# Keys, values and query squares turned by VectorE blocks and a trip through memory instead of TensorE transposes

## The chip, the cores and the metric

The kernel runs on one core of a Trainium2 chip. The time is the device time in microseconds of one execution. Below, PE is TensorE's matmul stream and PEld its weight loads, DVE is VectorE, ACT is ScalarE, POOL is GpSimd and SP is SyncE, which issues most DMAs. Each engine works through its own list of instructions in order; an instruction that has to wait holds all that stand behind it on that engine.

## The reference: what is computed

One layer of a hybrid streaming encoder for 2048 prompt rows and 8 running streams of 16 rows, 1024 wide. After a norm and a product with `w_in`, one half of the mixer is a gated delta rule with 4 heads of 128, the other half a short gated convolution; then come the output product, a norm and a SwiGLU feed-forward part. The lines that matter here:

```
qkv, conv_new = causal_dwconv(qkv_in, conv_prev, conv_qkv_w)
qkv = jax.nn.silu(qkv.astype(jnp.float32))
q = l2norm(q by heads) * 128 ** -0.5 ;  k = l2norm(k by heads)
A = where(strict, (k * beta) @ k.T * decay, 0)           # per chunk and head
sol = triangular_solve(eye + A, [v * beta, k * beta * exp(g)])
S, o = scan over chunks: v_new = u - w @ S;  o = qg @ S + qk @ v_new
       S = S * exp(g_last) + k_tail.T @ v_new
```

The l2norm needs, for each row and head, the sum of squares of 128 numbers. The chunk steps need keys and values with rows on partitions, while the convolution produces them with channels on partitions, so a block of keys or values has to be turned.

## The kernel before

The work has a first phase (input product, convolutions, delta rule, gated convolution) and later ones (output product, feed-forward). The change touches the first phase alone.

The 17 row tiles of 128 rows form five groups of 4, 4, 3, 3 and 3 tiles (group 3 has the running streams' tile). For each group the main loop goes through 28 blocks of `w_in` columns in the order of `SEQS`: key, value, query and gate blocks of four heads each ("k", "v", "q", "z"), and the three kinds C, H and B of the gated convolution. A block is 24 matmuls into a PSUM bank (L326; the weights as high and low halves), issued in three thirds. After each third the loop runs the functions that are filed in the table `events` under that number, so a group has 84 places, 0 to 83. `PLAN` holds the numbers for the delta rule's steps: gate rates and sums, key norms, pair products, the solve's load and store, the levels a, b, c/d, and the chunk steps. `TURNS` holds, for kinds k, q and v and for each head, at which number the block is turned. The weights come as 1 MB loads (L296, from a split copy in memory) into three buffers: SP issues each when PE has released the buffer.

A finished block goes through `finish_block`: ACT copies the bank (R, L335) and makes the first convolution tap (acc, L367), DVE adds the other three (L330), ACT applies SiLU (L374: kT, qT or vraw). For k, q and v it returns one function `later`, filed under the number of `TURNS`. That function calls `turned` (L384): one TensorE transpose per tile into a PSUM bank (tbank). For k, `sumsq` squares the bank on ACT and sums on DVE (L390), and ACT copies the bank to `kt` (L409). For q only the squares' sums are taken. For v, ACT scales each tile by a row factor `rt` on its way to `vt` (L427).

The pair products (L597, L604) leave AU, from which DVE solves 32x32 triangular systems for all heads: it multiplies and subtracts small tiles (`pr`, L631, and `Ts`, L633) in 31 steps that shrink to 16 wide, and turns the result with two 32x32-block transposes (L638, L639: `utd`). Level a (L650) multiplies the turned blocks on TensorE, so it waits for L638 and L639. Levels b to d build the inverse further, and the chunk steps use it with `kt`, `vt` and the queries (from L768).

What stands between the steps of the solve on DVE (convolution taps, sums, copies for the next group's norm) is set by the order in which the program's scheduler places the instructions of all events on that engine.

## Time and profile before

| | us |
|---|---|
| median of 3 runs | 2420.13 (2420.04 to 2421.8) |
| profiled execution, its own time | 2421.49 |
| profiled execution, span of its instructions | 2419.5 |
| first phase, groups 0 to 4 start at about | 7, 189, 392, 546, 700 |
| PE busy in the span | 2402.4 |

The span is what the trace shows from the first to the last instruction; the execution's own time is 2 us longer. In rows of groups of instructions, the columns are line, engine, operation, names of output and input (buffer numbers left out), shape and count, then busy time, mean duration and idle time ahead of it. In timeline rows the first number is the start from the beginning of the span, the second the duration; "x8" is eight instructions in one row. PE's matmuls overlap in the pipeline: their own durations add up to more than the time they take.

### The profile page before, as it was taken

How to read it: one execution, taken by the hardware profiler on the slowest of the kernel's cores; microseconds unless marked ns; L12 is line 12 of the kernel's file. 1: busy time of each engine (PE TensorE's matmuls, PEld its weight loads, DVE VectorE, ACT ScalarE, POOL GpSimd, SP SyncE). 2: the span in 40 equal slices, each digit the busy share in tenths (PEclk: the TensorE clock that was granted, in tenths of full speed). 3: DMA queues.
4: the chain of work that ended last, by engine and by line, in shares of the span. 5: the costliest groups of instructions: out<-in, count | busy, mean ns of one | idle time of the engine just before them, and what ended most of it. 6: DMA issues, size and time to landing. Idle time of an engine off the chain costs nothing.

```text
span 2419.5 us, 39078 instructions
## 1 busy us (share of the span) xinstructions
PE 2402.4 (99%) x14222; PEld 2204.9 (91%) x14222; DVE 1603.4 (66%) x3042; ACT 1064.3 (44%) x2367; POOL 561.3 (23%) x667
## 2 busy tenths in 40 slices
PE   9999999999999999999999999999999999999998
PEld 7888889999989988899999999999999988888877
DVE  7875755746667466888788744546456555666787
ACT  6645545546445445543444423334333345333443
POOL 1211001001110000256555200000000035455663
PEclk9999999999999999999999999999999999999999
DMA  8774655766777668599888888888988844334376
GB/s 289 259 245 170 221 192 195 251 216 240 259 260 248 243 177 240 208 339 296 271 280 267 287 254 254 256 261 271 311 297 282 253 154 129 101 120 127 118 235 205
DMA packets 317063, 561.36 MB, mean 232 GB/s; under 512 B 95940, under 2 KB 198536, under 8 KB 299592
## 3 DMA queue, kind: packets, MB, share of 16 engines
q1 hardware_dynamic: 216864, 490.66, 61.1%
q10 hardware_dynamic: 99784, 67.17, 9.0%
q8 instruction: 112, 1.84, 0.3%
q0 software_dynamic: 224, 1.05, 0.1%
q14 instruction: 79, 0.65, 0.1%
HBM read 400.09 MB, written 158.70 MB: 231 GB/s over the span
## 4 chain that ended last, share of the span: by engine, by line
PE 93%; DVE 3%; ACT 1%; DMA 1%; POOL 1%; issue 1%; POOLq 0%; SPq 0%; DVEq 0%; ACTq 0%
PE fbank L1446 36%; PE dbank L326 25%; PE fbank L1637 17%; PE dbank L1200 4%; PE ftbank L1200 4%; PE tbank L384 1%; PE gbank L597 1%; PE gbank L604 1%; PE obank L776 1%; PE gbank L768 1%; PE gbank L790 1%; PE obank L798 1%; PE gbank L784 1%; DVE sA L1413 0%; PE gbank L701 0%
## 5 line engine op out<-in xcount | busy, mean ns | idle before, releaser
L1446 PE MATMUL fbank<-xh,fw 128*128 128x384 f32 (+1 forms) x3696 | 898.2, 326 | 2.7 <-ACT m L1479 1.7
L1446 PEld LDWEIGHTS fbank<-xh,fw 128*128 128x128 f32 x3696 | 651.2, 188 | 5.0 <-ACT m L1478 2.7
L326 PE MATMUL dbank<-hi,w 128*128 128x384 f32 (+1 forms) x2224 | 650.8, 363 | 0.2 <-ACT w L1008 0.2
L1446 PE MATMUL fbank<-xl,fw 128*128 128x384 f32 (+1 forms) x1848 | 602.1, 326 | 0.0
L326 PEld LDWEIGHTS dbank<-hi,w 128*128 128x128 f32 x2224 | 409.6, 188 | 40.4 <-issue 4.5
L1637 PE MATMUL fbank<-dw,as 128*128 128x512 f32 x1785 | 416.1, 391 | 2.5 <-ACT as L1617 1.1
L1637 PEld LDWEIGHTS fbank<-dw,as 128*128 128x128 f32 x1785 | 334.6, 188 | 76.9 <-ACT as L1617 1.5
L326 PE MATMUL dbank<-lo,w 128*128 128x384 f32 (+1 forms) x1112 | 396.7, 357 | 0.3 <-DVE lo L241 0.3
L1446 PEld LDWEIGHTS fbank<-xl,fw 128*128 128x128 f32 x1848 | 346.9, 188 | 0.0
L326 PEld LDWEIGHTS dbank<-lo,w 128*128 128x128 f32 x1112 | 209.3, 188 | 16.0 <-DVE lo L241 0.6
L1620 POOL TENSOR_TENSOR as<-ar,as 128x256 fp32r<-128x256 f32 (+1 forms) x202 | 173.8, 869 | 182.3 <-ACT as L1617 170.4
L1617 ACT CAST as<-ar 128x256 fp32r<-128x256 f32 (+1 forms) x287 | 119.0, 427 | 203.1 <-PE fbank L1637 154.9
L1590 DVE TENSOR_TENSOR acc<-acc,fbank 128x512 f32<-128x512 f32 x219 | 148.0, 683 | 86.7 <-PE fbank L1637 68.5
L1285 POOL TENSOR_TENSOR dw<-dr,dw 128x512 fp32r<-128x512 f32 x48 | 67.7, 1418 | 513.8 <-ACT dw L1283 513.4
L1421 ACT CAST fw<-rg 128x512 fp32r<-128x512 f32 x124 | 77.2, 622 | 223.3 <-PE fbank L1446 136.8
L330 DVE SCALAR_TENSOR_TENSOR acc<-R,vec,acc 128x512 f32<-128x512 f32 (+2 forms) x180 | 120.8, 673 | 26.8 <-ACT acc L367 20.9
L1494 DVE TENSOR_TENSOR c<-u,fbank 128x384 f32<-128x384 f32 (+1 forms) x66 | 34.9, 528 | 98.1 <-PE fbank L1446 98.1
L1490 DVE TENSOR_TENSOR m<-m,m 128x384 f32<-128x384 f32 (+1 forms) x44 | 23.1, 526 | 81.3 <-ACT m L1480 81.2
L1497 ACT ACTIVATE c<-c 128x384 f32<-128x384 f32 (+1 forms) x66 | 33.4, 506 | 95.3 <-DVE c L1496 95.3
L1422 POOL TENSOR_TENSOR fw<-rg,fw 128x512 fp32r<-128x512 f32 x44 | 65.9, 1499 | 34.1 <-ACT fw L1421 34.0
L1492 ACT ACTIVATE m<-fbank 128x384 f32<-128x384 f32 (+1 forms) x66 | 31.2, 473 | 94.0 <-PE fbank L1446 70.2
L359 POOL COPY hist<-R 128x3 f32<-128x3 f32 x60 | 18.4, 307 | 217.9 <-ACT R L335 172.3
(402 smaller groups left out, 3558.2 us busy)
## 6 DMA issues: line engine op xcount, KB each, us to landing
w<-wsplit SPq DMA_DIRECT2D x105, 1024.0 KB, 5.1
fw<-fsplit SPq DMA_DIRECT2D x188, 512.0 KB, 4.8
fsplit<-fw SPq DMA_DIRECT2D x94, 512.0 KB, 4.3
partd<-pt ACTq DMA_DIRECT2D x86, 384.0 KB, 6.3
rg<-in_w_gu SPq DMA_DIRECT2D x62, 512.0 KB, 4.3
wsplit<-w SPq DMA_DIRECT2D x28, 1024.0 KB, 4.9
ar<-partd SPq DMA_DIRECT2D x43, 384.0 KB, 3.2
wr<-in_w_in SPq DMA_DIRECT2D x32, 512.0 KB, 6.2
```

The source lines that it names most:

```text
L326: T.matmul(ps[:, :c], l[:, k, :], r[k][:, :c], start=(k == 0 and r is hi and l is wh), stop=(k == KD - 1 and l is wl))
L330: r = V.scalar_tensor_tensor(acc, raw(d), w[:, d:d + 1], acc, op0=ALU.mult, op1=ALU.add)
L1200: T.matmul(pss[n], m_[:, j, :], w_[k][:, n * 512:(n + 1) * 512], start=(k == 0 and ci == 0), stop=(k == KD - 1 and ci == 2))
L1285: e.tensor_tensor(out=w[1], in0=v, in1=w[0].bitcast(F32), op=ALU.subtract)
L1421: A.copy(w[:, 0], v)
L1422: e.tensor_tensor(out=w[:, 1], in0=v, in1=w[:, 0].bitcast(F32), op=ALU.subtract)
L1446: T.matmul(ps, w_[:, c], b_[k][:, :hw], start=(first and k == 0 and ci == 0), stop=(k == KH - 1 and ci == 2), skip_group_check=not first)
L1494: V.tensor_add(c21, u2, b3)
L1590: mark_d["V"] = V.tensor_tensor(out=dst if out is None else out, in0=dst, in1=ps, op=ALU.add)
L1617: ins = mark_d["A"] = A.copy(a[:, 0, :n], v)
L1620: mark_d["V" if e is V else "G"] = e.tensor_tensor(out=a[:, 1, :n], in0=v, in1=a[:, 0, :n].bitcast(F32), op=ALU.subtract)
L1637: ins = T.matmul(ps, a[:, x_, q * P:(q + 1) * P], w[y_], start=(start and q == 0 and ci == 0), stop=(q == c - 1 and ci == 2), skip_group_c ...
```

## The change

Three things are altered for each group.

*Keys and values.* `turn_out` lets DVE turn the block's 32x32 squares in place of a full transpose (STREAM_TRANSPOSE of the whole block, into `kt` or `vt`), and SP stores the result in four DMAs, one for each quarter of the partitions, to a scratch tensor `turnd` in memory, with runs of 32 floats (128 bytes) set so that the tensor holds rows by channels. `turn_in` loads it back with rows on partitions. Then `key_sums` squares on ACT and sums on DVE from `kt`, and `value_scale` scales `vt` in place on ACT. The three functions of a block have three numbers in `TURNS`, some 3 apart.

*Query squares.* `query_parts` turns the block's squares on DVE, squares it on ACT and sums runs of 32 on DVE into `pq`; `query_sums`, once per group, adds the four parts with four matmuls against small identities (`eyes`) into one bank, which DVE copies to `ssq`.

*Plan.* `turned`, `sumsq` and their TensorE transposes are gone. The numbers for the key norms move to 33, 31 and 24 (from 32, 26 and 17), group 1's chunk steps from 66 to 68.

```diff
@@ -40,14 +40,18 @@
         [16, 17, 18, *range(0, 4), *range(8, 12), *range(12, 16), *range(4, 8), *range(19, 28)],
         [*range(0, 4), *range(8, 12), *range(12, 16), *range(4, 8), *range(16, 28)])
 LATE = (*SEQS[0][:2], 7, 11, 19, 23, 27)
-PLAN = {0: (14, 20, 22, 26, 32, 36, 40, 50, (67, 69, 71), 75),
-        1: (16, 20, 23, 28, 26, 33, 38, 51, (56, 58, 60), 66),
-        2: (8, 14, 17, 22, 17, 28, 32, 47, (52, 55, 58), 63),
-        3: (8, 14, 17, 22, 17, 28, 32, 47, (53, 56, 59), 64),
-        4: (8, 14, 17, 22, 17, 28, 32, 47, (52, 55, 57), 62)}
-TURNS = ({"k": (19, 19, 31, 31), "q": (43, 43, 55, 55), "v": (52, 52, 64, 64)},
-         {"k": (17, 20, 23, 26), "q": (33, 33, 39, 39), "v": (55, 55, 61, 61)},
-         {"k": (14, 14, 17, 17), "q": (28, 28, 31, 31), "v": (46, 46, 52, 52)})
+PLAN = {0: (14, 20, 22, 26, 33, 36, 40, 50, (67, 69, 71), 75),
+        1: (16, 20, 23, 28, 31, 33, 38, 51, (56, 58, 60), 68),
+        2: (8, 14, 17, 22, 24, 28, 32, 47, (52, 55, 58), 63),
+        3: (8, 14, 17, 22, 24, 28, 32, 47, (53, 56, 59), 64),
+        4: (8, 14, 17, 22, 24, 28, 32, 47, (52, 55, 57), 62)}
+TURNS = ({"k": ((11, 14, 17), (14, 17, 20), (19, 22, 26), (25, 28, 31)), "q": ((33,), (38,), (55,), (61,)),
+          "v": ((46, 49, 52), (52, 55, 58), (58, 61, 64), (64, 67, 70))},
+         {"k": ((17, 19, 22), (20, 22, 25), (22, 25, 28), (25, 27, 30)), "q": ((29,), (32,), (35,), (38,)),
+          "v": ((52, 55, 58), (55, 58, 61), (58, 61, 64), (61, 63, 65))},
+         {"k": ((8, 11, 14), (11, 14, 17), (14, 17, 20), (17, 20, 23)), "q": ((21,), (24,), (27,), (30,)),
+          "v": ((43, 46, 49), (46, 49, 52), (49, 52, 55), (52, 55, 58))})
+QSUM = (66, 42, 34)
 TLS = True
 O_SPLIT = 7
 NPD, NPT, NPG = 3, 2, 2
@@ -129,6 +133,7 @@
     mixo = [dram.tile([P, H, P], F32, name=f"mixo{t}") for t in range(NT)]
     mixs = [dram.tile([P, 4, len(g) * P], F32, name=f"mixs{gi}") for gi, g in enumerate(GROUPS)]
     wsplit = [dram.tile([P, 2, KD, P], F32, name=f"wsplit{j}") for j in range(28)]
+    turnd = {(kind, gi): dram.tile([H, len(g) * P, P], F32, name=f"turn{kind}{gi}") for kind in "kv" for gi, g in enumerate(GROUPS)}
     hTd = [dram.tile([4 * len(g), 32, D] if gi else [D, len(g) * P], F32, name=f"hTd{gi}") for gi, g in enumerate(FGROUPS)]
     partd = [[dram.tile([len(g) // 2, P, 7, len(c) // 2, P], F32, name=f"partd{gi}_{ch}") for ch, c in enumerate(FCHUNKS)]
              for gi, g in enumerate(FGROUPS)]
@@ -378,17 +383,47 @@
             if rb is not None:
                 flush()
 
-        def turned(src, n):
-            ps = tbank()
-            for i in range(n):
-                T.transpose(ps[:, i * P:(i + 1) * P], src[:, i * P:(i + 1) * P], ident)
-            return ps, ps[:, :n * P].rearrange("p (t d) -> p t d", d=P)
-
-        def sumsq(ps, n, ss, h):
+        def turn_out(g, kind, h, src):
+            n, dst = g["n"], g[kind + "t"][:, h]
+            V.transpose(dst[:, :n].rearrange("p t d -> p (t d)"), src[:, :n * P])
+            for a in range(4):
+                r = slice(32 * a, 32 * a + 32)
+                with tc.issue_after(wloads[-1].ins):
+                    nc.sync.dma_start(out=turnd[kind, g["gi"]][h, :, r].rearrange("(j c) f -> c j f", c=32),
+                                      in_=dst[r, :n].rearrange("c t (j f) -> c (t j) f", f=32))
+
+        def turn_in(g, kind, h):
+            with tc.issue_after(wloads[-1].ins):
+                nc.sync.dma_start(out=g[kind + "t"][:, h, :g["n"]], in_=turnd[kind, g["gi"]][h].rearrange("(t p) d -> p t d", p=P))
+
+        def key_sums(g, h):
+            n = g["n"]
             sq = cp.tile([P, W1], F32, tag="cs", name="sq")
-            A.activation(sq[:, :n * P], ps[:, :n * P], AF.Square)
-            V.tensor_reduce(out=ss[:, :4 * n].rearrange("p (t h) -> p h t", h=H)[:, h], in_=sq[:, :n * P].rearrange("p (t d) -> p t d", d=P),
-                            axis=AX.X, op=ALU.add)
+            A.activation(sq[:, :n * P].rearrange("p (t d) -> p t d", d=P), g["kt"][:, h, :n], AF.Square)
+            V.tensor_reduce(out=g["ssk"][:, :4 * n].rearrange("p (t h) -> p h t", h=H)[:, h],
+                            in_=sq[:, :n * P].rearrange("p (t d) -> p t d", d=P), axis=AX.X, op=ALU.add)
+
+        def query_parts(g, h, src):
+            c = g["n"] * P
+            if not h:
+                g["pq"] = small.tile([P, 4, MAXT, H], F32, tag="pq", name="pq", bufs=1)
+            qb = cp.tile([P, W1], F32, tag="vraw", name="qb", bufs=NKV)
+            V.transpose(qb[:, :c], src[:, :c])
+            A.activation(qb[:, :c], qb[:, :c], AF.Square)
+            V.tensor_reduce(out=g["pq"][:, :, :g["n"], h].rearrange("p j t -> p t j"),
+                            in_=qb[:, :c].rearrange("p (t j f) -> p t j f", j=4, f=32), axis=AX.X, op=ALU.add)
+
+        def query_sums(g):
+            m = 4 * g["n"]
+            ps = bank()
+            for j in range(4):
+                T.matmul(ps[32 * j:32 * j + 32, :m], eyes, g["pq"][:, j, :g["n"]].rearrange("p t h -> p (t h)"), start=True, stop=True)
+            V.tensor_copy(g["ssq"][:, :m], ps[:, :m])
+
+        def value_scale(g, h):
+            for i in range(g["n"]):
+                v = g["vt"][:, h, i]
+                A.activation(v, v, AF.Copy, scale=g["rt"][:, 4 * i + h:4 * i + h + 1])
 
         def sm(nm, w=4 * MAXT):
             return small.tile([P, w], F32, tag=nm, name=nm)
@@ -403,29 +438,18 @@
                 conv_qkv(tiles, 4 + h, ps, o, rb)
                 g["kT"].append(o)
 
-                def later():
-                    tb, t3 = turned(o, n)
-                    sumsq(tb, n, g["ssk"], h)
-                    A.copy(g["kt"][:, h, :n], t3)
-                return later
+                return [lambda: turn_out(g, "k", h, o), lambda: turn_in(g, "k", h), lambda: key_sums(g, h)]
             if kind == "q":
                 o = gp.tile([P, W1], F32, tag="qT", name="qT", bufs=H)
                 conv_qkv(tiles, h, ps, o, rb)
                 g["qT"].append(o)
 
-                def later():
-                    tb, _ = turned(o, n)
-                    sumsq(tb, n, g["ssq"], h)
-                return later
+                return [lambda: query_parts(g, h, o)]
             if kind == "v":
                 raw = cp.tile([P, W1], F32, tag="vraw", name="vraw", bufs=NKV)
                 conv_qkv(tiles, 8 + h, ps, raw, rb)
 
-                def later():
-                    _, t3 = turned(raw, n)
-                    for i in range(n):
-                        A.activation(g["vt"][:, h, i], t3[:, i], AF.Copy, scale=g["rt"][:, 4 * i + h:4 * i + h + 1])
-                return later
+                return [lambda: turn_out(g, "v", h, raw), lambda: turn_in(g, "v", h), lambda: value_scale(g, h)]
             if kind == "z":
                 src = ps[:, :c]
                 if rb is not None:
@@ -885,6 +909,7 @@
                 at(pairs + 3 * (i // 2) + i % 2 - 1, decay_scale, g, i)
                 at(pairs + 3 * (i // 2), pair_keys, g, i)
                 at((52, 42, 33)[min(gi, 2)] + 3 * (i // 2), pair_queries, g, i)
+            at(QSUM[min(gi, 2)], query_sums, g)
             at(load, solve_load, g)
             for b in range(4):
                 at(load + 2 + 3 * b * (store - load - 2) // 13, solve, g, range(8 * b, min(31, 8 * b + 8)))
@@ -1038,6 +1063,10 @@
             if k == 2:
                 fetch()
                 held = [mark["cast"], mark["rest"]]
+        eyes = gp.tile([P, 32], F32, name="eyes")
+        for b in range(4):
+            r = slice(32 * b, 32 * b + 32)
+            G.tensor_copy(eyes[r], ident[r, r])
         gps = gate_matmuls(raws, c)
         matmuls(firsts[2], pending[2][1:], hi, lo, c, range(6))
         with tc.issue_after(ins.ins):
@@ -1104,10 +1133,9 @@
                     if not early:
                         matmuls(ps, w, hi, lo, c, ks)
                     if s == 2:
-                        later = finish_block(j, ps, g)
-                        if later:
-                            kind, h = BLOCKS[j]
-                            events.setdefault(TURNS[min(gi, 2)][kind][h], []).insert(0, later)
+                        kind, h = BLOCKS[j]
+                        for t, f in zip(TURNS[min(gi, 2)].get(kind, ((),) * 4)[h], finish_block(j, ps, g) or ()):
+                            events.setdefault(t, []).insert(0, f)
                         if gi or slot not in (2, 3):
                             with tc.issue_after(mark["rb"].ins), tc.issue_after(mark["E"].ins) if not gi and slot < 2 else ExitStack():
                                 fetch()
```

The order of instructions on the engines changes with it. Three places follow; in each the first list is from before, the second from the changed kernel.

ACT in group 2, where the value blocks are finished: `vraw` is the SiLU of a value block, `vt` the scaling of a turned one (three tiles per head), `cs` a copy for the gated convolution, `xt` squares for the next group's norm.

```order
L374 ACTIVATE vraw<-acc 128x384
L261 ACTIVATE xt,xss<-xt 128x512 x2
L427 ACTIVATE vt<-tbank,rt 128x128 x6
L335 COPY R<-dbank 128x384
L367 ACTIVATE acc<-dbank,vec 128x384
L374 ACTIVATE vraw<-acc 128x384
L441 COPY cs<-dbank 128x384
L374 ACTIVATE vraw<-acc 128x384
```

```order
L266 ACTIVATE xt,xss<-xt 128x512 x2
L340 COPY R<-dbank 128x384
L372 ACTIVATE acc<-dbank,vec 128x384
L379 ACTIVATE vraw<-acc 128x384
L426 ACTIVATE vt<-vt,rt 128x128 x3
L465 COPY cs<-dbank 128x384
L379 ACTIVATE vraw<-acc 128x384
```

The first scaling of a value block, which waited for PE's bank, now waits for the first `turn_in` load, and still stands ahead of the last value block's SiLU.

DVE in group 2, the end of the solve up to its two transposes:

```order
L631 TENSOR_TENSOR pr<-As,Ts 128x96
L330 SCALAR_TENSOR_TENSOR acc<-R,vec,acc 128x384
L633 TENSOR_TENSOR Ts<-Ts,pr 128x8x12
L330 SCALAR_TENSOR_TENSOR acc<-R,vec,acc 128x384
L631 TENSOR_TENSOR pr<-As,Ts 128x91
L633 TENSOR_TENSOR Ts<-Ts,pr 128x7x13
L631 TENSOR_TENSOR pr<-As,Ts 128x78
```

```order
L655 TENSOR_TENSOR pr<-As,Ts 128x108
L657 TENSOR_TENSOR Ts<-Ts,pr 128x9x12
L655 TENSOR_TENSOR pr<-As,Ts 128x96
L657 TENSOR_TENSOR Ts<-Ts,pr 128x8x12
L655 TENSOR_TENSOR pr<-As,Ts 128x91
L388 STREAM_TRANSPOSE vt<-vraw 128x384
L657 TENSOR_TENSOR Ts<-Ts,pr 128x7x13
L655 TENSOR_TENSOR pr<-As,Ts 128x78
```

The fourth value block's transpose, which needs the SiLU from the ACT list above, stands seven steps before the solve's end; the other three stand at earlier steps of the same solve.

DVE in group 3, the last rows of the solve (`u` is the product of the first C and H blocks):

```order
L631 TENSOR_TENSOR pr<-As,Ts 128x16
L633 TENSOR_TENSOR Ts<-Ts,pr 128x16
L638 STREAM_TRANSPOSE utd<-Ts 128x32x16
L639 STREAM_TRANSPOSE utd<-utd 128x512
L450 TENSOR_TENSOR u<-cs,dbank 128x256
L456 TENSOR_TENSOR u<-cs,dbank 128x8x16
```

```order
L474 TENSOR_TENSOR u<-cs,dbank 128x256
L480 TENSOR_TENSOR u<-cs,dbank 128x8x16
L657 TENSOR_TENSOR Ts<-Ts,pr 128x4x14
L481 COPY sch<-u 128x16
L655 TENSOR_TENSOR pr<-As,Ts 128x45
L657 TENSOR_TENSOR Ts<-Ts,pr 128x3x15
L655 TENSOR_TENSOR pr<-As,Ts 128x30
L335 SCALAR_TENSOR_TENSOR acc<-u,vec,acc 128x400
L657 TENSOR_TENSOR Ts<-Ts,pr 128x2x15
L335 SCALAR_TENSOR_TENSOR acc<-u,vec,acc 128x400
L655 TENSOR_TENSOR pr<-As,Ts 128x16
L657 TENSOR_TENSOR Ts<-Ts,pr 128x16
```

The product `u`, which reads the H block's bank, and two of its taps moved ahead of the solve's last steps and its transposes.

## The prediction

> **What bounds the kernel now.** I read the page first, then the waits of TensorE (PE) in the first phase, then the timelines round the places where the change takes work away.
>
> ```profile
> span 2419.5 us, 39078 instructions
> PE 2402.4 (99%) x14222; PEld 2204.9 (91%) x14222; DVE 1603.4 (66%) x3042; ACT 1064.3 (44%) x2367; POOL 561.3 (23%) x667
> PEclk9999999999999999999999999999999999999999
> PE 93%; DVE 3%; ACT 1%; DMA 1%; POOL 1%; issue 1%; POOLq 0%; SPq 0%; DVEq 0%; ACTq 0%
> ```
>
> PE is busy 99% of the span, at full clock in every slice, and holds 93% of the chain of waits. The change lies in the first phase, five groups. By group (core line left out; columns: PE, PEld, DVE, ACT, POOL busy, clock, DMA share, GB/s):
>
> ```profile
> 7.00:189.00 182.00, 180.94 (x1115) 149.60 (x1116) 143.53 (x284) 107.97 (x186) 27.98 (x41) 1.00 0.75 259
> 189.00:392.00 203.00, 203.00 (x1314) 171.62 (x1312) 122.48 (x284) 104.96 (x242) 16.23 (x40) 1.00 0.53 194
> 392.00:546.00 154.00, 153.91 (x1149) 150.86 (x1149) 92.72 (x246) 78.61 (x204) 15.43 (x42) 1.00 0.66 230
> 546.00:700.00 154.00, 152.85 (x1150) 145.75 (x1150) 98.86 (x291) 76.70 (x200) 20.47 (x58) 1.00 0.71 247
> 700.00:860.00 160.00, 159.66 (x1181) 154.04 (x1180) 98.80 (x259) 78.98 (x186) 11.99 (x35) 1.00 0.71 247
> ```
>
> The groups begin at about 7, 189, 392, 546 and 700 us. In each, PE is idle for at most 1.2 us, while VectorE (DVE) is busy 60 to 79% and the DMA engines 53 to 75%. So an instruction taken off PE shortens the phase, unless PE then waits for another engine. PE's waits from 8 to 865 us, the longest first:
>
> ```profile
> PE gbank L845 <- ACT qT L842: 0.8, 1, 0.8
> PE gbank L527 <- DVE gg L519: 0.4, 1, 0.4
> ```
>
> Little is waited for; the next question is how near the others are to being waited for.
>
> **The change part by part.** *Removed from PE: 204 transposes (L384).* One shows 0.27 us, but they overlap, so I take the distance from the first of a set to the next instruction's start:
>
> ```profile
> 746.89 0.82 PE L384 MATMUL tbank<-cst,qT 128*128 128x128 f32 x6
> 747.55 0.72 PE L597 MATMUL gbank<-kT 128*128 128x128 f32 x5
> ```
>
> Six take 0.66 us, 0.11 each: 204 x 0.11 = **-22.4 us**, 48 of them (5.3) in groups 0 and 1 each and 36 (4.0) in the others. (By the Trainium skill, "VectorE: DVE Perf Modes", The three transpose paths, a 128x128 transpose costs TensorE 390 ns and VectorE 311; the distance here is less than a third of the first, so the figure is not used.)
>
> *Added to PE: four small matmuls per group for the query sums.* Nearest rows:
>
> ```profile
> L527 PE MATMUL gbank<-gg,masks x10: 175/258/285, 49.8 to 725.5; 128*128 128x16 f32 x4, 128*128 128x12 f32 x4, 128*128 128x8 f32 x2
> 483.43 0.95 PE L650 MATMUL gbank<-utd,AU 32*32 32x32 f32 x48
> ```
>
> Between 0.02 us each (48 small ones in 0.95) and 0.26 (alone): 0.1 to 1.0 us per group. I take 0.5, so **+2.5 us** (0.5 to 5).
>
> *Where PE can be made to wait.* Level a (L650) reads what DVE's triangular solve leaves (transposes L638, L639). The end of L638 against PE's start of L650, groups 0 to 4 (DVE rows, then PE rows; group 2's PE row is above):
>
> ```profile
> 145.26 1.17 DVE L638 STREAM_TRANSPOSE utd<-Ts 128x512 f32<-128x512 f32 x1
> 318.42 1.13 DVE L638 STREAM_TRANSPOSE utd<-Ts 128x512 f32<-128x512 f32 x1
> 482.14 1.14 DVE L638 STREAM_TRANSPOSE utd<-Ts 128x512 f32<-128x512 f32 x1
> 632.54 1.16 DVE L638 STREAM_TRANSPOSE utd<-Ts 128x512 f32<-128x512 f32 x1
> 787.18 1.12 DVE L638 STREAM_TRANSPOSE utd<-Ts 128x512 f32<-128x512 f32 x1
> ...
> 148.50 1.20 PE L650 MATMUL gbank<-utd,AU 32*32 32x32 f32 x64
> 320.73 0.95 PE L650 MATMUL gbank<-utd,AU 32*32 32x32 f32 x48
> 634.48 0.69 PE L650 MATMUL gbank<-utd,AU 32*32 32x32 f32 x32
> 788.45 0.95 PE L650 MATMUL gbank<-utd,AU 32*32 32x32 f32 x48
> ```
>
> Slack: 2.07, 1.18, 0.15, 0.78, 0.15 us. In two groups there is none, and DVE is full just ahead of it. The change puts DVE work into this solve; the prices:
>
> ```profile
> 460.00:475.00 15.00, 15.00 (x91) 14.97 (x90) 14.16 (x45) 5.99 (x16) 1.11 (x6) 1.00 0.74 269
> L639 DVE STREAM_TRANSPOSE utd<-utd x5: 674/711/712, 146.9 to 788.3; 128x512 f32<-128x512 f32 x5
> L390 DVE TENSOR_REDUCE ssq<-sq x20: 544/554/689, 101.6 to 755.0; 128x3 f32<-128x384 f32 x12, 128x4 f32<-128x512 f32 x8
> ```
>
> A 128x512 transpose is 0.71, about 0.6 back to back; I scale a 128x384 one to 0.53. No idle time takes them in: DVE is busy 14.16 of the 15 us ahead of the join.
>
> Group 2 (and 4): four value transposes, 2.1 us, and a copy and two small operations, 0.3, enter; the solve starts 0.85 earlier, since the query reduces no longer stand ahead; PE arrives 0.9 earlier (12 transposes less, matmuls added). Late: 2.4 - 0.85 + 0.9 - 0.15 = 2.3 us, on DVE's work alone.
> Group 1: two transposes 1.2 and a copy against two reduces 1.4, PE 1.9 earlier, slack 1.2: 0.7 to 1.1.
> Group 0: six transposes 3.9, a weight remainder 1.2 and an output pair 1.3 enter, two reduces and a tap (2.1) leave, so +4.5 with the copy; PE comes 3.0 earlier (32 transposes less, 0.5 added), slack 2.07: 5.4. And three key transposes now stand ahead of gg, for which PE already waited 0.4: +2.0. Together 7.4.
> Group 3: the first H block's product u and its two taps now stand ahead of the solve's last transpose, and that block ends right before level a. Before, they came after:
>
> ```profile
> 634.66 0.42 DVE L450 TENSOR_TENSOR u<-cs,dbank 128x256 f32<-128x256 f32 x1 [0.22 <-PE dbank L326]
> 637.54 1.30 DVE L330 SCALAR_TENSOR_TENSOR acc<-u,vec,acc 128x400 f32<-128x400 f32 x2 [0.49 <-ACT acc L458]
> ```
>
> From the block's end at 634.4: u to 635.2, ScalarE's (ACT) product 0.7, the last tap to 637.3, the transpose 1.2: level a at 638.5, 4 us after 634.48. With the rest, 4.3 to 5.
>
> *The round trip through memory.* A turned value block is stored in four pieces of 128-byte runs, loaded back, and scaled by ACT (L426). In group 2 ACT's first scale stands ahead of the copy cs and of the last value block's SiLU; DVE's fourth value transpose waits for that SiLU, and the rest of the solve stands behind it. So a DMA landing enters the chain to PE. Before, at that place (ACT, then DVE):
>
> ```profile
> 474.07 1.66 ACT L427 ACTIVATE vt<-tbank,rt 128x128 f32<-128x128 f32 x6 [0.52 <-PE tbank L384]
> 479.60 0.48 ACT L441 COPY cs<-dbank 128x384 f32<-128x384 f32 x1 [2.60 <-PE dbank L326]
> 479.98 0.53 ACT L374 ACTIVATE vraw<-acc 128x384 f32<-128x384 f32 x1
> 479.20 0.24 DVE L631 TENSOR_TENSOR pr<-As,Ts 128x78 f32<-128x78 f32 x1
> ```
>
> The same kind of store stands later in this trace (128-byte runs), with four on SyncE (SP) in a row; then a load of the size wanted:
>
> ```profile
> L1231 SPq DMA_DIRECT2D hTd<-ht x24: 318/564/2863, 873.7 to 931.4; - x24
> DMA to landing us min/median/max: 3.1/4.3/5.5
> 873.71 4.02 SPq L1231 DMA_DIRECT2D hTd<-ht  x4
> xk<-in_xT SPq DMA_DIRECT2D x18, 192.0 KB, 5.0
> ```
>
> The first value transpose ends at about 469.6, three thirds of a block before the scale of 474.07. Lower bound: issues 4 x 0.32, landing 3.1, load issue 0.3 and 3.1: back at 477.4, before the scale's slot near 478 (three thirds of a block, 4.4 us, after the first scale of before), nothing lost. Upper bound: issues 4.0, landing 4.3, load 5.0 and 0.3: 483.2. Then three scales 0.83, cs 0.38, SiLU 0.53, transpose 0.53, and the 4.1 us of solve from 479.20 to 483.28: L638 would end at 489.6, and PE, there at 482.5, waits 7. I take the middle of 2.3 and 7, rather to the low side since the store here is 96 KB and not 128: **4** in groups 2 and 4, **5** in group 3, where the late H block covers part. The Trainium skill ("DMA: Bandwidth & Descriptors", Specifications) states that transfers under 512 bytes are read-modify-written and miss the line rate. The trace speaks against a large effect: the 128-byte stores land in 4.3 us where the 192 KB load takes 5.0. By the same page's fixed 2.0 us per DMA (Anatomy of one DMA) the trip would be about 6 us and hidden; this trace's own minimum is 3.1 for one of the two.
>
> *Other additions, at nothing:* the key path. Its stores and loads are further ahead of their users; if late, the key sums delay the norms by as much. The weight loads share SP:
>
> ```profile
> w<-wsplit SPq DMA_DIRECT2D x105, 1024.0 KB, 5.1
> SPq L296 <- PE dbank L326: 372.8, 78, 8.2
> ```
>
> SP waits 4.8 us on average for PE before it issues one, two blocks ahead of its use; four stores ahead of it cost up to 4.0. The waiting covers it; without that cover each late load costs PE the excess. ACT loses 20 copies and gains squares of the same size.
>
> **Sum.** 2421.5 (the profiled execution; its span is 2419.5) - 22.4 + 2.5 + stalls (7.4 + 1.0 + 4 + 5 + 4 = 21.4) = 2423.0. The runs' median, 2420.13, is 1.4 lower than the profiled execution: **2422 us**, no change that can be told. Within 0.2% is 2415.3 to 2425.0, about what a measurement of this kernel tells from no change.
>
> **Rivals.** *The cover holds (faster).* Loads come back at the minimum and DVE's added work falls into gaps; only group 3's wait, fixed by its order, stays: 2420.1 - 22.4 + 2.5 + 4.3 = 2405. For it: DVE idles 40% of groups 2 to 4 as a whole. Against it: slack 0.15 at the join, where DVE is full. With half of the stalls, 10.7, it is 2411.
> *The round trip decides (slower).* Upper bounds of it: 7 in groups 2, 3 and 4; in group 0, where the DMA share is highest, 12, since there too the scale of one value block stands ahead of another's SiLU; 3 in group 1: 36 us, 2420.1 - 22.4 + 2.5 + 36 = 2436. It decides from a landing of the first scale's load later than about 478 in group 2, each microsecond costing one in each of four groups. For it: landings of 4.3 and 5.0 as medians. Against: their minimum of 3.1.
> *The weights run late (slower).* Where the stores of two heads, 8.0 us of SP, stand ahead of one weight load, they exceed SP's mean wait of 4.8 by 3.2; at half of the ten such pairs of value heads that is 16 us on the forecast, 2438. SP's 372.8 us of waiting and the two blocks of lead speak against it. That the change does not do what it says I give no room: the transposes are gone from PE's list.
>
> **How the numbers follow.** Forecast 0.35 (2415 to 2428; 0.27 of it within 0.2%, 0.02 faster, 0.06 slower); cover holds 0.32; round trip decides 0.28; weights late 0.05. Faster 0.34, same 0.27, slower 0.39. Two in ten left out at the ends: 2403 to 2436; the forecast's own range is 2415 to 2428.
>
> **What would show it.** Right: no L384 for keys, values and queries on PE, five query-sum sets under 1 us; PE waits at level a on DVE's transposed block of 4 us or more in groups 0, 2, 3 and 4, and near 1 in group 1; ahead of it DVE idle at the fourth value transpose for ACT, and ACT idle before the value scale for the DMA. Wrong: level a without waits; a value load that lands before its slot; waits of the main matmuls for weights.

## The result, and the profile after

The changed kernel takes 2456.49 us in the median of 4 runs (2454.6 to 2462.89) against 2420.39 for the kernel before (2420.04 to 2421.8): a ratio of 1.0153, 95% interval 1.0133 to 1.0173. It is 36 us slower. The forecast was no change, 2422, with a range of its own of 2415 to 2428 and, with the rivals, of 2403 to 2436; the result lies above both.

The page of the changed kernel, the rows that answer to those of before (span, busy time, clock, the chain by engine):

```profile
span 2456.3 us, 39073 instructions
PE 2399.6 (98%) x14058; PEld 2196.7 (89%) x14058; DVE 1632.5 (66%) x3107; ACT 1062.7 (43%) x2347; POOL 562.2 (23%) x671
PEclk9999999999999999999999999999999999999999
PE 84%; DVE 6%; ACT 3%; DMA 3%; issue 2%; POOL 1%; SPq 0%; POOLq 0%; DVEq 0%; ACTq 0%
```

PE holds 84% of the chain where it held 93%. The clock row shows 9 in every slice, as before; a slice is 61 us long and 9 stands for anything from 90% up, so this row cannot show what follows. PE's waits from 8 to 900 us (total, times, longest):

```profile
PE gbank L674 <- DVE utd L662: 15.9, 4, 6.1
PE gbank L420 <- DVE pq L413: 5.3, 1, 5.3
PE gbank L621 <- DVE AU L622: 4.7, 3, 2.1
PE dbank L331 <- DMA w<-wsplit: 4.7, 6, 1.7
PE gbank L420 <- DVE dt L629: 2.8, 3, 1.0
PE gbank L551 <- issue: 2.3, 1, 2.3
PE tbank L749 <- ACT o L744: 2.0, 1, 2.0
```

L674 is level a, L420 the query sums' matmuls, L621 the pair products, L551 the gate sums, L331 the blocks. With four small ones the list comes to 40.1 us; before, it came to 2.5. The stretches of the five groups as they lay before, in the columns of before (the last three numbers are PE's clock, the DMA share and GB/s; the changed kernel's groups start up to 28 us later, so the stretches only add up to the phase):

```profile
7.00:189.00 182.00, 170.07 (x1003) 138.92 (x1002) 144.00 (x282) 97.74 (x155) 23.36 (x38) 0.95 0.82 273
189.00:392.00 203.00, 198.22 (x1267) 166.53 (x1266) 124.93 (x288) 103.52 (x234) 17.87 (x40) 1.00 0.65 216
392.00:546.00 154.00, 146.13 (x1050) 139.81 (x1049) 93.47 (x248) 79.01 (x195) 14.63 (x39) 0.97 0.68 226
546.00:700.00 154.00, 146.71 (x1040) 142.09 (x1039) 98.12 (x284) 75.84 (x199) 18.36 (x50) 0.98 0.77 257
700.00:900.00 200.00, 191.48 (x1410) 180.02 (x1410) 125.21 (x326) 90.65 (x217) 17.06 (x49) 0.99 0.76 250
```

There is a second loss beside the waits: **the granted clock**, 1.00 in all five stretches before, is now 0.95, 1.00, 0.97, 0.98 and 0.99. Length times what is missing gives 9.1 + 0 + 4.6 + 3.1 + 2 = 18.8 us. Part of these stretches lies over a wait and costs nothing there. A block's matmuls on both sides of the 5.3 us wait in group 0, from PE's timeline:

```profile
147.34 0.39 PE L331 MATMUL dbank<-lo,w 128*128 128x512 f32 x1
153.28 0.31 PE L420 MATMUL gbank<-pq,eyes 128*32 128x16 f32 x8 [5.33 <-DVE pq L413]
154.97 0.63 PE L331 MATMUL dbank<-lo,w 128*128 128x512 f32 x1
```

The same matmul shows 0.39 us ahead of the wait and 0.63 behind it. Level a in the five groups, whose starts before stand in the prediction:

```profile
159.95 1.54 PE L674 MATMUL gbank<-utd,AU 32*32 32x32 f32 x64 [1.97 <-DVE utd L662]
335.02 1.20 PE L674 MATMUL gbank<-utd,AU 32*32 32x32 f32 x64 [0.94 <-DVE rh L223]
504.03 1.49 PE L674 MATMUL gbank<-utd,AU 32*32 32x32 f32 x48 [4.85 <-DVE utd L662]
661.54 1.06 PE L674 MATMUL gbank<-utd,AU 32*32 32x32 f32 x32 [6.08 <-DVE utd L662]
821.95 0.99 PE L674 MATMUL gbank<-utd,AU 32*32 32x32 f32 x48 [3.05 <-DVE utd L662]
```

Against 148.50, 320.73, 483.43, 634.48 and 788.45 they come 11.4, 14.3, 20.6, 27.1 and 33.5 us later: the loss grows by 11.4, 2.8, 6.3, 6.5 and 6.4 from one to the next. Of the solve's two last transposes, level a waits for the first alone (L638 before, L662 here): in group 4 it starts at 821.95, 0.15 us after L662's end (820.72 and 1.08), while the second, which began at 821.83 and takes 0.71, still runs. The books: waits 40.1 - 2.5 = +37.6, transposes -22.4, sums' matmuls about +1.2 (five sets of 0.24), clock at most +18.8. That is +35 for the first phase; the first feed-forward matmul starts at 1074.0 us against 1038.9, 35.1 later, and the rest of the 36.8 us of span is behind it. Where half clock lies over a wait it is counted twice here, some 4 us, so about 4 of the 35 us are left without an account.

The chain through memory in group 2, drawn in the prediction, is there. SP, ACT, DVE, in order of time:

```profile
485.78 2.05 SPq L392 DMA_DIRECT2D turnv<-vt  x4
489.93 4.18 SPq L392 DMA_DIRECT2D turnv<-vt  x4
494.22 0.41 SPq L397 DMA_DIRECT2D vt<-turnv  x1
...
497.29 0.99 ACT L426 ACTIVATE vt<-vt,rt 128x128 f32<-128x128 f32 x3 [4.22 <-DMA turnv<-vt]
498.54 0.52 ACT L379 ACTIVATE vraw<-acc 128x384 f32<-128x384 f32 x1
...
499.10 0.58 DVE L388 STREAM_TRANSPOSE vt<-vraw 128x384 f32<-128x384 f32 x1 [2.16 <-ACT vraw L379]
```

The first block's load is issued 8.4 us after its first store, behind the second block's four stores. ACT waits 4.2 us, and its first scaling starts 11.5 us after the first store's issue; the profile names the landing of a store as what ended the wait, and the load, issued at 494.22, is the other candidate. DVE then waits 2.2 us for the last SiLU. Whether that is what the change costs is for the experiments.

### The profile page after: what moved, and what is told of

Read it like the earlier page. It is cut to its first block, busy times and chain, and to the rows that moved or that the text cites. A ratio compares the mean times of both kernels' runs of the same rounds, so it can differ in the third digit from the quotient of the medians.

```text
span 2456.3 us, 39073 instructions
## 1 busy us (share of the span) xinstructions
PE 2399.6 (98%) x14058; PEld 2196.7 (89%) x14058; DVE 1632.5 (66%) x3107; ACT 1062.7 (43%) x2347; POOL 562.2 (23%) x671
## 4 chain that ended last, share of the span: by engine, by line
PE 84%; DVE 6%; ACT 3%; DMA 3%; issue 2%; POOL 1%; SPq 0%; POOLq 0%; DVEq 0%; ACTq 0%
PE fbank L1474 34%; PE dbank L331 20%; PE fbank L1665 16%; PE dbank L1228 4%; PE ftbank L1228 4%; DVE acc L335 1%; PE obank L800 1%; PE gbank L792 1%; ACT pk L644 1%; PE gbank L814 1%; PE gbank L621 1%; PE gbank L808 1%; DMA turnv<-vt 1%; PE obank L822 0%; DVE sA L1441 0%
## 5 line engine op out<-in xcount | busy, mean ns | idle before, releaser
L331 PE MATMUL dbank<-hi,w 128*128 128x384 f32 (+1 forms) x2224 | 657.6, 367 | 4.7 <-DMA w<-wsplit 4.7
L331 PEld LDWEIGHTS dbank<-hi,w 128*128 128x128 f32 x2224 | 416.6, 191 | 48.6 <-issue 7.4
L331 PE MATMUL dbank<-lo,w 128*128 128x384 f32 (+1 forms) x1112 | 400.8, 360 | 0.0
L331 PEld LDWEIGHTS dbank<-lo,w 128*128 128x128 f32 x1112 | 212.6, 191 | 16.1
L1450 DVE TENSOR_TENSOR fw<-rg,fw 128x512 fp32r<-128x512 f32 x80 | 55.3, 691 | 10.2 <-ACT fw L1449 7.0
```

What stands on the lines that cost most here:

```text
L331: T.matmul(ps[:, :c], l[:, k, :], r[k][:, :c], start=(k == 0 and r is hi and l is wh), stop=(k == KD - 1 and l is wl))
L1450: e.tensor_tensor(out=w[:, 1], in0=v, in1=w[:, 0].bitcast(F32), op=ALU.subtract)
```

## The experiments

Two theories went in. **A**: the trip through memory, in the chain to level a, costs the time, and a wait is followed by half clock. **B**: it is the general load of VectorE and the queues. A third, **C**, came up after the first eight runs: it is VectorE's added work, and its order, in the chains PE waits for.

**Values back on TensorE.**

```diff
-                return [lambda: turn_out(g, "v", h, raw), lambda: turn_in(g, "v", h), lambda: value_scale(g, h)]
+                return [lambda: old_value(g, h, raw)]      # transposes and scaling as before
```

> The changed kernel with the value blocks turned by TensorE again (68 transposes), keys and queries as in the change. Theory A, the value blocks' trip through memory sits in the solve that TensorE waits for, and each TensorE wait of 2 us or more is followed by a stretch at half clock: the waits at level a (16.8 us in the changed kernel) and their half-clock stretches go, 136 transposes stay saved (15.0 us); what remains is group 0's gate wait (2.3 plus 1.7 of half clock) and waits of about 5 at the pair products: 2413 to 2424. Theory B, it is the general load of VectorE and of the DMA queues (keys and queries included): at least two thirds of the loss stays, above 2440.

Measured: 2435.18 us, 1.0064 (1.0047 to 1.0081) of before. Of the changed kernel's 36 us, 21 go with the values, 15 stay with keys and queries. PE's two largest waits there, summed:

```profile
PE gbank L647 <- DVE AU L648: 6.7, 4, 3.4
PE dbank L331 <- DMA w<-wsplit: 3.1, 5, 1.6
```

Level a hardly waits (0.7 us), as A said, but the pair products wait 6.7 us for VectorE's scaled product AU. Neither range holds: the keys and queries cost 30 us gross, twice the 15 that their transposes save, in places that A had left small.

**Values alone.** The edit in words:

```diff
-"k" and "q" of the change, its PLAN
+"k" and "q" with TensorE transposes, PLAN of before; "v" as in the change
```

> The kernel before with only the value blocks turned the new way (its plan is that of before; values take the change's three numbers). Theory A: 7.5 us of transposes saved, level a waits of 12 to 17 us and 8 to 10 us of half clock added: 2432 to 2446, with the clock at half after level a in groups 2, 3 and 4. Theory B: a third of the added load, so about a third of the loss: 2425 to 2433 with level a waits under 2 us each.

Measured: 2449.51 us, 1.0124 (1.0109 to 1.0139), above even A's range:

```profile
PE gbank L700 <- DVE utd L688: 22.8, 4, 7.4
```

Nearly all of PE's waiting is at level a (22.8 us). So the parts alone cost +29 (values), and below +13 (keys) and +3 (queries), 45 together, against 36 for all: their waits overlap.

**The scaling behind the last SiLU.** This takes the load out of the chain of group 2 without taking out a DMA; the scalings' numbers in `TURNS` move back to match.

```diff
-            for i in range(g["n"]):
-                A.activation(v, v, AF.Copy, scale=...)
+            with tc.issue_after(mark["V3"].ins):           # the last value block's SiLU
+                for i in range(g["n"]):
+                    A.activation(v, v, AF.Copy, scale=...)
```

> The changed kernel with ScalarE's scaling of the value blocks ordered behind the SiLU of the last value block, so that no load stands ahead of it; every transpose, store and load stays. Theory A: in groups 2 to 4 the fourth value transpose is no longer late, level a waits fall from 14 us together to about 6 (VectorE's own added work, 2 each) and fall below the length that brings half clock in at least two of them, group 0 gains 3 to 6: 2430 to 2442. Theory B: within 4 us of the changed kernel's 2456.

Measured: 2455.39 us, 1.1 below the changed kernel and inside its spread, as B had it. Level a in groups 2 and 3:

```profile
504.74 0.95 PE L677 MATMUL gbank<-utd,AU 32*32 32x32 f32 x48 [1.33 <-DVE utd L665]
663.81 1.06 PE L677 MATMUL gbank<-utd,AU 32*32 32x32 f32 x32 [6.20 <-DVE utd L665]
```

In group 2 the wait fell from 4.85 to 1.33, so the chain was real there; but waits of 1.5 for weights and 2.0 a little later took its place. In group 3 nothing changed, and in group 4 the wait stayed 3.04; in group 0 the wait at the query sums grew from 5.33 to 7.06. Theory A falls as the account of the whole. DVE's timeline of this run names group 3's holder:

```profile
657.65 0.42 DVE L477 TENSOR_TENSOR u<-cs,dbank 128x256 f32<-128x256 f32 x1 [1.20 <-PE dbank L331]
660.99 0.63 DVE L335 SCALAR_TENSOR_TENSOR acc<-u,vec,acc 128x400 f32<-128x400 f32 x1 [1.89 <-ACT acc L485]
```

The H block's product and its tap, ahead of the solve's last steps, wait for PE and for ACT. The prediction had priced that.

**The product behind the solve, too.**

```diff
-                V.tensor_mul(u[:, 2:2 + pc], cs[:, :pc], ps[:, :pc])
+                with tc.issue_after(g["solved"].ins) if "solved" in g and not h else ExitStack():
+                    V.tensor_mul(u[:, 2:2 + pc], cs[:, :pc], ps[:, :pc])
```

> As the run with the scaling ordered late, and the first H block's product u ordered behind the solve's last transposes on VectorE, as it stood before the change. If the 6.2 us wait of group 3 comes from that product standing ahead of the solve: it falls to 2 to 3, with 3.4 instead of 6.8 us of half clock, the time to 2446 to 2451. If it comes from VectorE's four added transposes or from the trip: the wait stays above 5 and the time within 3 us of 2455.

Measured: 2453.95 us. In group 3 the wait fell from 6.20 to 1.65, so most of it came from that product. The time fell by 1.4 only, which the spread covers, so neither range fits as a whole: now PE waits 2.1 us for the next group's norm (xk) behind the delayed products, 2.7 at level a in group 2 and 7.9 at group 0's query sums. The waits move on; the sum hardly falls.

**No trip.** Stores and loads of keys and values are left out; keys and values are used misplaced.

```diff
-            for a in range(4): ... nc.sync.dma_start(out=turnd[...], in_=dst[...])
-            with tc.issue_after(wloads[-1].ins): nc.sync.dma_start(out=g[kind + "t"][...], in_=turnd[...])
```

> The changed kernel without the stores and loads of turned keys and values: the 32x32 squares are turned and then used where they lie, so keys and values are misplaced and the output is not the reference's. All VectorE, ScalarE and TensorE work and its plan stay. Theory A (the trip is the larger part): gate, weight and pair-product waits shrink, group 2's level a wait falls from 4.9 to about 2, groups 3 and 4 keep theirs, 2425 to 2440. Theory C (VectorE's added work and its order are the larger part): 2444 to 2456.

Measured: 2448.25 us, 1.0115 (1.0101 to 1.0129). Without the trip, its DMAs, queues and landings, 28 of the 36 us remain. The waits for weights are gone; level a still waits 17 us in all. C holds, in its range. The 8 us are a net figure and no clean price of the trip: the order of other instructions moved with it, the wait at the query sums of group 0 (5.3 us) is gone, and the one at the gates grew from 2.3 to 5.5.

**VectorE's turns alone.** To the kernel before, one 32x32-square transpose per value block is added, and overwritten.

```diff
                 def later():
+                    V.transpose(g["vt"][:, h, :n].rearrange("p t d -> p (t d)"), raw[:, :c])
                     _, t3 = turned(raw, n)
```

> The kernel before with one added instruction per value block: VectorE turns its 32x32 squares into the values' tile, which ScalarE then overwrites with the scaled TensorE transposes as before. No DMA and no ScalarE work is added. This prices VectorE's 2.1 us in the solve alone. Theory C: level a waits of 1.5 to 3 us appear in groups 2 and 4 and bring 3.4 us of half clock each, 2426 to 2434. If VectorE has room for it: within 3 us of 2420.

Measured: 2434.74 us, 1.0059 (1.0045 to 1.0073), just above C's range. Level a in groups 0, 2, 3 and 4:

```profile
151.95 1.36 PE L651 MATMUL gbank<-utd,AU 32*32 32x32 f32 x64 [2.20 <-DVE utd L639]
491.73 0.95 PE L651 MATMUL gbank<-utd,AU 32*32 32x32 f32 x48 [2.10 <-DVE utd L639]
645.15 0.69 PE L651 MATMUL gbank<-utd,AU 32*32 32x32 f32 x32 [2.32 <-DVE utd L639]
800.72 1.09 PE L651 MATMUL gbank<-utd,AU 32*32 32x32 f32 x48 [2.10 <-DVE utd L639]
```

In groups 2 and 4, where the slack was 0.15, four turns of 0.57 come out whole, as waits of 2.10: the solve has no room. In groups 0 and 3 the waits are longer than the turns less the slack; the rest of VectorE's list moved too, which was not followed further. The 20 turns cost 14 us, almost twice the 7.5 that the 68 value transposes could save.

**A stall put into the kernel before.** Copies of the solve's tile onto itself ahead of its last transposes, none in group 0, 8, 3, 6 and 14 in the others.

```diff
+            for _ in range((0, 8, 3, 6, 14)[g["gi"]]):
+                V.tensor_copy(g["Ts"], g["Ts"])
             V.transpose(td..., g["Ts"]...)
```

> The kernel before with copies of the solve's tile onto itself put in front of its last transposes: none in group 0, 8, 3, 6 and 14 in groups 1 to 4. Nothing else changes, so TensorE waits at level a by what the copies take beyond the slack. Theory A: waits of about 1 us leave the granted clock at 1.00 behind them; a wait of 2 to 4 us is followed by 3.4 us at half clock, one of 5 to 6 by 3.4 or 6.8, each costing half its length beside the wait. Rival: the half clock of the changed kernel has another cause (its DMAs or its VectorE load) and the clock stays at 1.00 behind all four waits.

Measured: 2446.82 us in one run (span 2444.7). Level a in groups 1 to 4, then the clock in stretches round each (third number from the end):

```profile
326.13 1.87 PE L652 MATMUL gbank<-utd,AU 32*32 32x32 f32 x64 [4.81 <-DVE utd L640]
493.27 0.95 PE L652 MATMUL gbank<-utd,AU 32*32 32x32 f32 x48 [1.40 <-DVE utd L640]
648.70 1.07 PE L652 MATMUL gbank<-utd,AU 32*32 32x32 f32 x32 [4.31 <-DVE xss L266]
811.48 1.49 PE L652 MATMUL gbank<-utd,AU 32*32 32x32 f32 x48 [6.45 <-DVE utd L640]
```

```profile
321.00:333.00 12.00, 7.19 (x78) 5.77 (x77) 8.14 (x16) 4.69 (x10) 0.98 (x3) 0.72 0.41 160
484.00:496.00 12.00, 10.61 (x107) 10.32 (x106) 10.79 (x32) 7.23 (x21) 0.78 (x3) 1.00 0.75 279
642.00:654.00 12.00, 7.69 (x62) 7.26 (x62) 8.96 (x26) 6.15 (x19) 1.80 (x4) 0.72 0.54 206
804.00:818.00 14.00, 7.55 (x73) 7.24 (x72) 10.95 (x23) 4.24 (x11) 0.73 (x2) 0.63 0.28 99
```

Behind 1.40 us the clock stays at 1.00. Behind 4.81 and 4.31 it is at half for 0.28 x 2 x 12 = 6.7 us, behind 6.45 for 10. No DMA and no turning was added, so the half clock follows PE's idling and not the change's other traffic; the rival of the expectation falls. The waits are 17.0 us, the span is 25.2 longer. By the blocks' starts, the wait of 1.40 put PE 1.3 us back, and those of 4.81, 4.31 and 6.45 put it 8.0, 6.9 and 9.1 back: in this one run, a wait of such a size costs about one and a half times its length.

**Matmuls of constants in the waits.** The counterpart, in the changed kernel.

```diff
+        def filler(n):
+            ...
+                with tc.issue_after(mark["PE"].ins):       # the last block matmul issued before
+                    for _ in range(n):
+                        T.matmul(ps[:, :512], ident, masks[:, :512], start=True, stop=True)
+            filler(0 if g["gi"] else 5)                    # in query_sums
+            filler((0, 0, 4, 5, 2)[g["gi"]])               # in level_a
```

> The changed kernel with matmuls of constants, whose results nobody reads, put on TensorE ahead of the waits it has: 5 ahead of group 0's query sums, 4, 5 and 2 ahead of level a in groups 2, 3 and 4; they fill part of waits of 5.3, 4.9, 6.1 and 3.1 us. If the half clock follows TensorE's idling and costs what the windows show (23.8 us at half there, some 10 lost): the time falls by 5 to 11 us to 2445 to 2451 and the clock stays at 1.00 at these places. If the half clock has another cause or costs nothing: 2455 to 2460.

Measured: 2449.45 us, 1.0118 (1.0102 to 1.0134): 7 us under the changed kernel's median by work that nobody needs (the two intervals just touch), in the range for a half clock that costs time. The clock round the query sums and round level a in groups 2, 3 and 4:

```profile
150.00:160.00 10.00, 6.01 (x28) 3.19 (x28) 9.62 (x28) 2.18 (x3) 0.32 (x3) 1.00 1.00 295
495.00:510.00 15.00, 14.13 (x203) 11.57 (x201) 11.10 (x34) 8.49 (x23) 0.96 (x4) 1.00 1.03 318
650.00:668.00 18.00, 16.29 (x157) 13.22 (x157) 10.46 (x33) 7.81 (x23) 1.39 (x6) 0.91 0.95 295
800.00:825.00 25.00, 23.68 (x263) 22.07 (x262) 20.85 (x58) 9.20 (x22) 1.71 (x8) 1.00 1.00 297
```

At three of the four filled places the clock now stays whole. In group 0 the wait moved to level a, right behind the stretch shown, and 3.4 us of half clock follow it there:

```profile
159.97 1.20 PE L683 MATMUL gbank<-utd,AU 32*32 32x32 f32 x64 [3.58 <-DVE utd L670]
```

By the blocks' starts, groups 0, 2, 3 and 4 gained 0.4, 3.1, 1.0 and 3.3 us. The missing clock of the phase fell from 18.8 to 10.2 us (six stretches of 3.4 us at half are left), the span by 8.9. Together with the stall this ties the half clock to PE's idling, and shows that it costs time.

**Keys alone, and queries alone.** Keys as in the change with its plan, queries and values on TensorE; queries as in the change with the plan of before. The edit in words:

```diff
-three kinds the new way
+"k" alone (first run), "q" alone (second run)
```

> The changed kernel with queries and values turned by TensorE again, so only the keys go through memory (with the change's plan). Theory A: the gate wait of 2.3 us and the pair-product wait of 3 us in group 0 with their half-clock stretches stay, and the wait of 2 us at the end of group 1 stays: 2424 to 2434. Theory B: about 2413 to 2418, the 7.5 us saved and little lost.

> The kernel before with only the query squares made the new way (plan of before, the change's numbers for queries). Keys and values together cost 15 us in group values-by-TensorE and 29 alone; this run and the next split what keys and queries do. Theory A (the loss outside the values is in the keys' trip through memory ahead of the pair products and of the gates in group 0): 2411 to 2418, 7.5 saved, 3 to 5 lost at the sums' matmuls. Theory B (it is the queries' added VectorE work): 2424 to 2434, most of it in group 0.

Measured: keys 2433.11 us, 1.0051 (1.0035 to 1.0066), in A's range; queries 2423.44 us, 1.0011 (1.0002 to 1.0020), just under B's range and, as B had it, lost in group 0. The keys keep the gate wait (2.4), a weight wait (2.9) and one of 2.0 at group 1's end. The queries are 4.7 us behind at the end of group 0, by the blocks' starts, after a wait of 2.8 at the pair products with its half clock and one of 1.4; in groups 2 to 4 the sums' matmuls wait 0.9 us each for VectorE's dt.

**Group 1's chunk steps at 68.**

```diff
-        1: (16, 20, 23, 28, 26, 33, 38, 51, (56, 58, 60), 66),
+        1: (16, 20, 23, 28, 26, 33, 38, 51, (56, 58, 60), 68),
```

> The kernel before with one number of its plan changed: group 1's chunk steps at 68 instead of 66, as the change has it. Theory: the chunk steps then reach into group 2's blocks, and the wait of 2.0 us for the gated output with 3.4 us at half clock near 433 us in the changed kernel comes from this number alone: 2423 to 2426. Rival: it comes from the added VectorE and ScalarE work, and this run stays within 1.5 us of 2420.

Measured: 2420.99 us, 1.0003 (0.9993 to 1.0012): the number alone costs nothing. What in the change makes PE wait 2.0 us (2.9 without the trip) for the gated output at group 1's end stays open; it is there in every run that has the new keys and this plan.

**Queries, tuned.** The aim here was a faster kernel. First, query turns in group 0 and all sums later; then group 0's turns forced behind the solve; then keys through memory from group 2 on.

```diff
-"q": ((33,), (38,), (55,), (61,)) in group 0, QSUM = (66, 42, 34)
+"q": ((43,), (46,), (55,), (61,)),            QSUM = (74, 62, 60)      # tuned
+"q": ((68,), (69,), (70,), (71,)) behind the solve's last transpose, QSUM = (74, 62, 60)   # late
```

> Queries alone made the new way, with group 0's first two query turns behind the pair products (43 and 46 in place of 33 and 38) and the sums' matmuls at 74, 62 and 60 in place of 66, 42 and 34, behind level a. In the run of queries alone the waits at these two places cost 4.6 us in group 0 and 1.4 in each of groups 2 to 4. If it is the waits and their half clock that ate the 7.5 us saved: 2412 to 2416, faster than both kernels. If the waits only move to level a: 2419 to 2426.

> As the tuned queries, and in group 0 all four query turns ordered on VectorE behind the solve's last transposes (numbers 68 to 71, the sums' matmuls at 74). The tuned run lost 5.8 us in group 0, with a 3.1 us wait at level a and 6.8 us of half clock, and gained 0.7 to 0.9 in each later group. If group 0's loss is these turns in the solve: 2414 to 2417. If it only moves to the chunk steps: 2419 to 2423.

> As the run with late queries, and keys through memory in groups 2 to 4 alone, where the run of keys alone gained 1.2 to 1.6 us in groups 3 and 4. If these gains add: 2 to 4 us under the run with late queries, 2411 to 2415. If VectorE cannot take both ahead of the pair products: no gain on it, or a loss of 1 to 3.

Measured: tuned 2421.82 us, 1.0004 (0.9995 to 1.0013), in the range for waits that only move: group 0's loss had moved to level a (3.1 us, then 6.8 us of half clock). Late: **2417.45 us, 0.9984 (0.9975 to 0.9993)**, just above its range, with no half clock in the first phase and no wait above 1.1 us:

```profile
PE tbank L389 <- ACT vraw L379: 1.1, 1, 1.1
PE gbank L752 <- DVE U L760: 0.8, 1, 0.8
```

This beats both kernels, by 3.8 us over the one before, of the 7.5 that its 68 transposes cost. With keys from group 2 on it is 2417.88, 0.9988 (0.9979 to 0.9997): no gain on top.

## Why the prediction was wrong

*The bound.* Right: PE set the phase, and the slack at level a was what it looked like. The turns added alone to the kernel before came out as waits of 2.1 to 2.3 us.

*The transposes, 0.11 us each.* Not contradicted. In groups 2 to 4 the late queries gain about 0.8 to 1.1 us each, from 12 transposes (1.3) less the sums' matmuls.

*The sums' matmuls, 0.5 per group.* Their own time is 0.24, but the term left out what they wait for: 5.3 us in group 0 and 0.95 in each of groups 2 to 4, for VectorE work that stands ahead of their input. 8.1 us of waits were missing from this term; in group 0 the sum had them in part as a stall at level a.

*The stalls at level a.* By place: forecast 5.4, 1.0, 4, 5, 4 (19.4), measured 1.97, 0.94, 4.85, 6.08, 3.05 (16.9), with group 0's stall taken mostly at the query sums instead: 5.33 there and 1.97 at level a, 7.3 against 5.4. The gate wait was forecast at 2.0 more, and is 2.3 against 0.4. So the part of the sum that was worked out from rows was near, in part by luck: the round trip, which the forecast put into these terms, had no part in groups 3 and 4, which the late scaling shows. In group 2 it took 11.5 us from the first store's issue to the first scaling, between the forecast's bounds of 7.8 and 13.6 (477.4 and 483.2 less 469.6). A store of the change is 48 KB there (32 partitions of 384 floats), where the forecast leaned to the low side for one of 96.

*The additions "at nothing".* Wrong: weights 4.7 us, pair products 4.7, the end of group 1 2.0. The key path was said to be "further ahead of their users"; the keys alone cost 13 us net, 20 gross.

*The price of a wait.* This is the step that failed most: the sum took each microsecond of wait as one. PE's clock was read as full in every slice and then left out of the argument, though every stall of the forecast made PE idle. The clock adds up to 18.8 us, about 15 of them outside the waits. Behind every wait of 3 us or more that nothing filled, and behind some from 1.65 us on, the matmuls run at half speed for 3.4, 6.8 or 10 us. By the Trainium skill ("TensorE: Matmul & The Clock Gate", Part 1) the clock goes to half after an idle window of some 3.4 us, and the window runs freely. The stretches here are multiples of 3.4 us, which agrees. Some waits of 1.65 to 2.3 us already bring them, below the 3 us that the same page of the Trainium skill gives as the gap to avoid (Why this matters for your kernels).

Put together: stalls 21.4 in the forecast and 37.6 measured, 16.2 more; missing clock up to 18.8. That is 35 us beside a miss of 34, of which some 4 are counted twice, so about 4 us of the miss stay open.

*The rivals.* "The round trip decides", 2436, was on the right side for the wrong reason: without the trip 28 of the 36 us remain. "The cover holds" is refuted by level a's waits. "The weights run late" was 4.7 us of the waits, not 16.

## What to carry to other kernels

Where PE is busy 99% and another engine's chain reaches it with no slack, moving work from PE to that engine is paid back at the join: 2.1 us of added VectorE work made a wait of 2.1 us, against 12 value transposes worth 1.3 us in that group. In this kernel a wait of PE above 4 us cost about one and a half times its length, since the clock dropped behind it; price such waits so, and look at the clock in stretches, since the page's row of slices hides it. And what can be placed behind the join, as the query turns could, gains; moving one holder out of the chain only brings up the next.

## What the runs showed of the hardware

Waits of PE of up to 1.4 us left the clock whole wherever they stood. Those of 1.65 to 2.5 us dropped it in some places and not in others. Level a's 1.65 us in group 3 of the run with the delayed product was followed by 3.4 us at half clock:

```profile
656.85 0.69 PE L678 MATMUL gbank<-utd,AU 32*32 32x32 f32 x32 [1.65 <-DVE utd L666]
655.00:662.00 7.00, 5.35 (x51) 5.11 (x50) 4.37 (x13) 4.52 (x12) 0.49 (x2) 0.76 1.09 295
```

The gate wait of 2.5 us in the run with the values on TensorE was followed by none; with the turns alone, 2.20 and 2.10 us in groups 0 and 4 were followed by 3.4 us at half clock, 2.10 and 2.32 us in groups 2 and 3 by none. Every wait of 3 us or more that nothing filled dropped it. Useless matmuls in four of the changed kernel's waits kept the clock up in three of these places and took 7 us off the median.
